# Another written order of TensorE's units in the mixer of a two-layer trunk

## The chip, the cores and the metric

The kernel runs on one core of one Trainium2 chip. The metric is the device time of one execution in microseconds (us), taken as the median of several. Engines are TensorE (PE; its weight loads are PEld), VectorE (DVE), ScalarE (ACT), GpSimd (POOL) and SyncE (SP), which issues most transfers. Each engine works through its own queue of instructions in order, and the queues wait for each other by semaphores.

## The reference

Two layers over 512 tokens of width 1024. Layer 0 has a mixer of two halves: an S5 state-space group and a stick-breaking attention with 8 heads of 64. Layer 1 is a convolution module. Both are followed by a layer norm and a feed-forward part. The change touches the mixer of layer 0 alone:

```python
h = x @ mix_w_in[i] + mix_b_in[i]
u, q, k, v = jnp.split(h, [S5_WIDTH, S5_WIDTH + SB_WIDTH, S5_WIDTH + 2 * SB_WIDTH], axis=-1)
s5_out = s5_mixer(u, ...)       # diagonal complex recurrence, gelu, gated product
sb_out = stick_breaking_attention(q.reshape(head_shape), k.reshape(head_shape), v.reshape(head_shape))
mix = jnp.concatenate([s5_out, sb_out], axis=-1) @ mix_w_out[i] + mix_b_out[i]
...
# stick-breaking attention, for each block of queries
z = jnp.einsum('bqhd,bkhd->bhqk', q_blk.astype(jnp.float32), kf) * scale
strict = key_pos[None, :] < q_pos[:, None]
log_beta = jax.nn.log_sigmoid(z)
log_keep = jnp.where(strict, jax.nn.log_sigmoid(-z), 0.0)
after = lax.cumsum(log_keep, axis=3, reverse=True) - log_keep
weights = jnp.where(strict, jnp.exp(log_beta + after), 0.0)
return jnp.einsum('bhqk,bkhd->bqhd', weights, vf)
```

## The kernel before

Activations lie transposed, features on the 128 partitions and the 512 tokens along the row. Large products are made from two-part splits: a value is kept as hi and lo, and each product of 128 x 128 by 128 x 512 is done three times (hi x hi, hi x lo, lo x hi). A projection of 128 columns therefore has 8 x 3 = 24 products (`gemm`, L219 to L227). The splitting of weights takes a cast on ACT (whi, L98 or L101) and a subtraction on DVE (wlo, L99 or L102); the raw weights come by SP (L71). Three slots hold split weights in the mixer, and a unit's weights are prepared up to two units ahead, with high priority.

The mixer is cut into units, and `ORDER` (L53) is the list of them. The loop at L798 goes through the list; it chains every TensorE instruction behind the one before it in the list (L804 to L808), so TensorE's order is written out by hand. The instructions of the other engines follow from the same tracing: a scheduler orders each of their queues by the order of tracing and by readiness, and hands out the buffers. So the list moves them too, though less strictly. The list also gives the order in which weights are fetched (L238 to L245).

The units:

- `q0` to `v3`: projection of head pair 0 to 3 (two heads each), into one of three shared PSUM banks ("mm"); ACT moves the result to SBUF (L644). There are two tiles of q, two of k and one of v.
- `aNs` with A, B or C: scores z of pair N for key blocks 0 (A), 1 and 3 (B), or 2 (C), both heads, into two of four "z" banks (L683). Behind them ACT takes the absolute value, exponential and logarithm, DVE combines (sp), POOL masks, and ACT and DVE split (sh, sl). The split tiles of A are single, those of B and C double, so one per head.
- `aNw` with A, B or C and the head: TensorE adds the running sums of the splits to z (L708), ACT takes the exponential into a w tile (three of them, tag "wt", shared with `yf`), POOL masks it (L672). A needs the splits of A, B and C, B those of B and C, and C those of B and C; the products with a block's own split come last.
- `aNt`: v transposed (vt, one tile); `aNv` with A, B or C: weighted values, L723, into the only bank "av"; `aNe`: the split of av into ch (ACT) and cl (DVE), tiles that the output projection reads.
- `G0` to `G3`: tables of a quarter of the S5 groups: DVE makes Gx and Cx, TensorE transposes (gp, L522) and multiplies (tp, L532), ACT copies to gt and tk, and SP lays tk out as Tx with sixteen copies (L539). `s`: states; TensorE makes vR and vI from gt (L547, L549), DVE runs the scan over tiles that share six places (tag "sp") and ends with the two halves of Sx. `y`: outputs yp from Tx, Cx and Sx (L577, L579), which DVE adds to U.
- `e0` to `e3`: gelu (ACT with the Tanh table, DVE), out and back through HBM by five transfers on SP (yf), and a split. A table of ACT is loaded whenever the kind of function changes in the order of tracing.
- `r`: clears a tile `rows` on POOL (it shares the six "sp" places) and loads the bias and norm vectors into it with fourteen loads on SP (L628); `R`: transposes it.
- `l0` to `l3`: gated product of S5; `o0` to `o7`: the first half of the output projection (acmo), with the result added to X by DVE.

Behind the mixer comes `tail_norm_lead` (L1019): the other half of the output projection, from the attention's splits (tiles `tla`), the sum and mean for the layer norm (`sa` on DVE, `mpa` on TensorE, L915), then the feed-forward part. Its weight buffers take memory that the mixer gives back.

## Time and profile before

| what | value |
|---|---|
| median of 3 runs | 1202.27 us (1202.24 to 1204.54) |
| the profiled execution | 1201.93 us, span 1200.2 us |
| TensorE busy | 1166.2 us of the span |
| VectorE, ScalarE, GpSimd busy | 755.8, 505.5, 61.4 us |
| mean granted TensorE clock | 0.988 |

The span is the time from the first to the last instruction of the profiled execution. The profile lists each engine's idle time by what ended it ("z1C <- ACT sh1B" is a TensorE instruction that writes z1C and started when ACT's sh1B was there), and it gives the share of full speed that TensorE's clock was granted in any stretch of time (PEclk). Names of tiles are the program's; z0A is the score tile of pair 0, blocks A.

### The profile page before, as it was taken

Reading aid. Unit: us, or ns where it says so; the run is one execution under the profiler, and the core shown is the slowest. Engines: PE = TensorE matmul, PEld = TensorE weight load, DVE = VectorE, ACT = ScalarE, POOL = GpSimd, SP = SyncE. Lnnn points to the kernel's source line nnn. Section 1 sums busy time; section 2 is a strip of 40 time slices with the busy share of each in tenths; the row PEclk is TensorE's granted clock in tenths of the full one; section 3 lists DMA queues with packets and bytes.
Section 4 is the critical chain, followed back from the end, with each engine's and each line's share of the span. In section 5 each row is a group of like instructions: output and inputs, shape, how many; then the busy total and the mean of one; then the engine's idle time right before and its main releaser. Section 6 shows DMA issues by size and latency. Waiting matters only on the chain.

```text
span 1200.2 us, 17726 instructions
## 1 busy us (share of the span) xinstructions
PE 1166.2 (97%) x7148; PEld 973.7 (81%) x7148; DVE 755.8 (63%) x1342; ACT 505.5 (42%) x798; POOL 61.4 (5%) x125
## 2 busy tenths in 40 slices
PE   9998999999999999999999999899999999999997
PEld 7776877789888888888899776599988888888885
DVE  7997885478635545545555899887843434444446
ACT  6854779334524424425323132553642331423220
POOL 1021111000000000000021110002000000000000
PEclk9998999999999999999999999999999999999999
DMA  8611321150778787887554642206142241323211
GB/s 203 177 43 31 88 67 62 53 176 17 265 249 279 260 281 265 269 288 260 183 170 158 235 140 72 73 1 211 55 146 81 93 134 57 120 74 120 70 53 70
DMA packets 132546, 169.58 MB, mean 141 GB/s; under 512 B 13874, under 2 KB 105778, under 8 KB 132464
## 3 DMA queue, kind: packets, MB, share of 16 engines
q1 hardware_dynamic: 123664, 136.96, 35.3%
q0 software_dynamic: 8640, 31.46, 7.7%
q8 instruction: 56, 0.92, 0.3%
q14 instruction: 26, 0.21, 0.1%
q10 hardware_dynamic: 160, 0.03, 0.0%
HBM read 132.12 MB, written 35.65 MB: 140 GB/s over the span
## 4 chain that ended last, share of the span: by engine, by line
PE 74%; DVE 9%; DMA 7%; issue 4%; ACT 4%; POOL 1%; SPq 0%; DVEq 0%; ACTq 0%; POOLq 0%
PE f L225 16%; PE g L1311 12%; PE acf L225 9%; PE fl L225 5%; DMA raw<-in_ffn_w_dram 5%; PE tld L225 4%; PE tlb L225 4%; PE pv L225 3%; PE h L1295 3%; DVE wlo L102 3%; PE pg L225 3%; PE cw L1126 2%; PE acmo L225 2%; PE pl L225 2%; ACT whi L101 1%
## 5 line engine op out<-in xcount | busy, mean ns | idle before, releaser
L102 DVE TENSOR_TENSOR wlo<-raw,whi 128x1024 fp32r<-128x1024 f32 x176 | 213.2, 1224 | 200.4 <-ACT whi L101 197.9
L101 ACT CAST whi<-raw 128x1024 fp32r<-128x1024 f32 x176 | 181.9, 1049 | 326.0 <-PE g L1311 106.9
L1311 PE MATMUL g<-whi,hl 128*128 128x512 f32 x208 | 81.6, 392 | 0.0
L1311 PE MATMUL g<-whi,hh 128*128 128x512 f32 x208 | 81.6, 392 | 0.0
L1311 PE MATMUL g<-wlo,hh 128*128 128x512 f32 x208 | 81.5, 392 | 0.0
L225 PE MATMUL f<-xah,whi 128*128 128x512 f32 x208 | 81.0, 390 | 0.0
L225 PE MATMUL f<-xdh,whi 128*128 128x512 f32 x208 | 81.0, 389 | 0.0
L225 PE MATMUL f<-xdh,wlo 128*128 128x512 f32 x208 | 80.9, 389 | 0.0
L225 PE MATMUL f<-xal,whi 128*128 128x512 f32 x208 | 80.9, 389 | 0.0
L225 PE MATMUL f<-xdl,whi 128*128 128x512 f32 x208 | 80.9, 389 | 0.0
L225 PE MATMUL f<-xah,wlo 128*128 128x512 f32 x208 | 80.9, 389 | 0.0
L225 PE MATMUL acf<-hl,whi 128*128 128x512 f32 x192 | 75.5, 393 | 0.2 <-DVE hl L216 0.2
L225 PE MATMUL acf<-hh,whi 128*128 128x512 f32 x192 | 75.6, 394 | 0.0
L225 PE MATMUL acf<-hh,wlo 128*128 128x512 f32 x192 | 75.4, 393 | 0.0
L215 ACT CAST hh<-fr 128x512 fp32r<-128x512 f32 x64 | 39.7, 621 | 60.6 <-DVE fr L353 60.6
L216 DVE TENSOR_TENSOR hl<-fr,hh 128x512 fp32r<-128x512 f32 x64 | 44.1, 690 | 31.8 <-ACT hh L215 31.7
L357 DVE SCALAR_TENSOR_TENSOR cy<-hp,wdw,cy 128x512 f32<-128x512 f32 (+1 forms) x81 | 52.2, 646 | 0.0
L353 DVE TENSOR_TENSOR fr<-fr 128x512 f32<-128x512 f32 x64 | 43.7, 685 | 13.4 <-ACT fr L154 13.4
L357 DVE SCALAR_TENSOR_TENSOR cz<-hp,wdw,cz 128x512 f32<-128x512 f32 (+1 forms) x74 | 47.6, 644 | 0.0
L1311 PEld LDWEIGHTS g<-whi,hl 128*128 128x128 f32 x208 | 39.0, 188 | 8.7
L1311 PEld LDWEIGHTS g<-wlo,hh 128*128 128x128 f32 x208 | 39.1, 188 | 8.7
L1311 PEld LDWEIGHTS g<-whi,hh 128*128 128x128 f32 x208 | 39.0, 188 | 8.8
(631 smaller groups left out, 2874.5 us busy)
## 6 DMA issues: line engine op xcount, KB each, us to landing
raw<-in_ffn_w_dram SPq DMA_DIRECT2D x48, 1024.0 KB, 5.5
raw<-in_ffn_w_dram SPq DMA_DIRECT2D x32, 512.0 KB, 3.6
kepth<-whi SPq DMA_DIRECT2D x30, 512.0 KB, 5.9
keptl<-wlo SPq DMA_DIRECT2D x30, 512.0 KB, 10.4
whi<-kepth POOLq DMA_DIRECT2D x30, 512.0 KB, 3.5
wlo<-keptl POOLq DMA_DIRECT2D x30, 512.0 KB, 4.6
raw<-in_conv_w_pw_dram SPq DMA_DIRECT2D x12, 1024.0 KB, 6.3
raw<-in_mix_w_in_dram SPq DMA_DIRECT2D x16, 512.0 KB, 4.8
```

Source lines behind the costliest of these rows:

```text
L101: i0 = nc.scalar.copy(hi, raw).ins
L102: i1 = nc.vector.tensor_sub(lo, raw, hi.bitcast(F32)).ins
L215: i0 = S.copy(hi, src).ins
L216: i1 = V.tensor_sub(lo, src, hi.bitcast(F32)).ins
L225: ins = PE.matmul(ps[:, c0:c1], u[:, k, ksl], v[:, c0:c1], start=start and k == 0 and i == 0, stop=stop and k == n - 1 and i == 2).ins
L353: V.tensor_tensor(o, x, y, op=op)
L357: V.scalar_tensor_tensor(o, x, s, y, op0=op0, op1=op1)
L1126: PE.matmul(cps[j, c0][g][C, :], Ds[j][t // 16][R, t % 16, :], hps[j][R, t + c0 : t + c1], start=t < 4, stop=t >= n - 4, tile_position=(R. ...
L1295: PE.matmul(ps, u, v, start=k == 0 and i == 0, stop=k == nk - 1 and i == 2)
L1311: PE.matmul(pss[b], u, v[:, kk, :], start=k + kk == 0 and i == 0, stop=k + kk == nb - 1 and i == 2)
```

## The change

The list of units gets another order. The units are the same and each is unchanged.

- Pair 0: `a0sB` and `a0sC` stand together, with `a0t`, `q1`, `k1`, `y0` behind them; then the weighings `a0wB0 a0wC0 a0wC1 a0wB1`, and `a0sA` behind these rather than between.
- `r` moves ahead of `G1`.
- `a0wA1` and `a0vB` directly follow `v1`; `a1sC`, `a1sB` and `y1` come after; `q2` and `a0vA` precede both `a1wC0` and `a1wC1`.
- `k2` goes ahead of `v2`, with `a1wB0`, `a0e` and `a1t` between; `y2`, `a1vB` and `e1` go ahead of `a1wA0`, `a2sB` ahead of `a1wA1`.
- `a2vC` goes ahead of `a2sA`.
- `a3vB`, `a3vA`, `a3e` go ahead of `o6` and `o7`.

The diff, with the lists broken into lines and the common beginning and the common stretches left out:

```diff
 q0 k0 v0 G0 s0 a0sB
-q1 a0sC k1 a0t y0 a0wC0 a0wC1 a0sA a0wB0 a0wB1 a0vC G1 s1 a0wA0 v1 a1sC a0wA1 a0vB r a1sB y1 a0vA a1wC1 q2 a0e a1wC0
+a0sC a0t q1 k1 y0 a0wB0 a0wC0 a0wC1 a0wB1 a0sA a0vC r G1 s1 a0wA0 v1 a0wA1 a0vB a1sC a1sB y1 q2 a0vA a1wC0 a1wC1
 e0 G2 a1sA s2
-a1t v2 k2 a1wB0 a1wB1 a1wA0 a1vC e1 y2 a1wA1 a2sB a1vB q3
+k2 a1wB0 a0e a1t v2 a1wB1 a1vC y2 a1vB e1 a1wA0 a2sB a1wA1 q3
 a1vA a1e e2 G3 a2sC s3 k3 a2wB1 a2t a2wC0 a2wC1
-a2sA a2wB0 a2vC
+a2vC a2sA a2wB0
 R y3 e3 v3
 ...
 o0 o1 o2 o3 o4 o5
-o6 o7 a3vB a3vA a3e
+a3vB a3vA a3e o6 o7
```

## The prediction

> **What bounds the kernel now.** I read the page's shares first, then TensorE's waits over the whole run, then busy time and granted clock in stretches laid around the longest waits, and last the order of time at each of them.

> ```profile
> span 1200.2 us, 17726 instructions
> PE 1166.2 (97%) x7148; PEld 973.7 (81%) x7148; DVE 755.8 (63%) x1342; ACT 505.5 (42%) x798; POOL 61.4 (5%) x125
> ```

> TensorE is busy for 97% of the span. So work of another engine counts only where TensorE waits for it. The waits (total, times, longest):

> ```profile
> PE z1C L708 <- ACT sh1B L215: 2.9, 1, 2.9
> PE av L723 <- POOL w2C L672: 2.5, 1, 2.5
> ...
> PE vR L547 <- ACT gt L524: 1.9, 2, 1.0
> ...
> PE z0A L683 <- ACT w0C L160: 1.4, 1, 1.4
> PE tla L225 <- DVE cl L216: 1.4, 1, 1.4
> ...
> PE mpa L915 <- DVE sa L353: 0.8, 1, 0.8
> PE v L225 <- DVE m L353: 0.6, 1, 0.6
> ```

> Five of these seven lie in the mixer; tla and mpa stand just behind it. A written order can take away such waits and nothing else, since every multiplication stays. The clock makes some of them dearer than they look:

> ```profile
> core 0: us, PE busy (x) PEld busy (x) DVE busy (x) ACT busy (x) POOL busy (x), PEclk, DMA share, GB/s
> 76.00:84.00 8.00, 7.25 (x48) 5.44 (x48) 7.31 (x16) 5.33 (x12) 1.76 (x5) 0.79 0.22 66
> 82.00:103.00 21.00, 19.73 (x132) 14.45 (x128) 19.59 (x35) 11.09 (x25) 4.44 (x10) 1.00 0.14 38
> 105.00:114.00 9.00, 7.71 (x22) 6.16 (x23) 5.97 (x13) 1.32 (x3) 0.36 (x1) 0.62 0.00 0
> 164.00:172.00 8.00, 5.46 (x39) 4.16 (x37) 6.34 (x15) 6.15 (x10) 1.24 (x4) 1.00 0.24 70
> 241.00:247.00 6.00, 4.62 (x26) 4.63 (x27) 1.18 (x2) 1.36 (x2) 0.00 (x0) 0.72 0.82 268
> 322.00:600.00 278.00, 277.69 (x1271) 229.68 (x1270) 146.93 (x165) 109.99 (x129) 0.00 (x0) 1.00 0.76 261
> ```

> The width times what is missing from the clock is what a stretch lost to it: 8 x 0.21 = 1.68 us behind the wait of z0A, 9 x 0.38 = 3.42 behind that of z1C, 6 x 0.28 = 1.68 behind that of tla. The 2.5 us of waiting in 164:172 cost no clock. The second row shows the danger: VectorE is busy for 19.59 of 21 us there, so TensorE can't run far ahead of it.

> **The change, part by part.** No instruction is added or removed. The rows of the places (start, duration, instruction, idle time before it):

> ```profile
> 76.75 1.40 PE L683 MATMUL z0A<-q,k 64*128 64x512 f32 x4 [1.45 <-ACT w0C L160]
> 98.11 1.13 PE L683 MATMUL z1B<-q,k 64*128 64x384 f32 x6 [0.31 <-ACT w0A L160]
> 99.17 0.49 PE L577 MATMUL yp<-U,Tx 128*128 128x128 f32 x2
> ...
> 102.05 1.08 PE L723 MATMUL av<-w0A,vt 128*64 128x512 f32 x4
> 105.99 0.43 PE L708 MATMUL z1C<-sh1B,negs 128*128 128x128 f32 x1 [2.86 <-ACT sh1B L215]
> 106.71 0.48 PE L708 MATMUL z1C<-sl1B,negs 128*128 128x128 f32 x1 [0.30 <-DVE sl1B L216]
> ...
> 164.39 0.33 PE L708 MATMUL z2B<-sh2B,negs 128*128 128x128 f32 x1
> ...
> 165.57 0.65 PE L723 MATMUL av<-w2C,vt 128*64 128x256 f32 x2
> 168.76 0.65 PE L723 MATMUL av<-w2C,vt 128*64 128x256 f32 x2 [2.54 <-POOL w2C L672]
> ...
> 242.38 0.41 PE L225 MATMUL tla<-ch,whi 128*128 128x256 f32 x1 [1.40 <-DVE cl L216]
> ```

> *Pair 0: both early scores, then a0t, q1, k1, y0; the weighings B0 C0 C1 B1; then a0sA.* Before, a0sA asked for two score banks right behind the two C weighings and waited 1.45 for the exponential of w0C. After, the first two banks come free behind B0 and C0, and C1 and B1 stand between. One B weighing takes 1.18 (164.39 to 165.57) and with C1 covers the wait. Gone: 1.45 + 1.68 = **3.13**. Two things are late next. q1 takes the bank of vR two units earlier than k1 did, so VectorE must have read it: between 0 and one 128x512 operation of 0.69 (row of cl, below); 0.1, because the reads of vR are the first that VectorE does there. And a0wB0 wants the B and C splits of its head together: between 0 and one weight split of 1.23 (row of wlo, below) in front of them on VectorE; 0.4, since two projections and y0 lie in between, but VectorE is full.

> *a0wA1 and a0vB ahead of a1sC and a1sB; q2 and a0vA ahead of a1wC0 and a1wC1.* Before, the C weighing of pair 1 had y1 and a0vA as cover, 99.17 to 103.13; sl1B came at 106.71, 7.5 after the scores' end at 99.24. After, y1 (2.9), a whole projection and a0vA (1.1) stand there. A projection has 24 products, at the pace of the row below (21.80 for 96) 5.45:

> ```profile
> 215.99 21.80 PE acmo L225 x96
> ```

> 2.9 + 5.45 + 1.1 = 9.4 covers 7.5 with 1.9 to spare. Gone: 2.86 + 0.30 + 3.42 = **6.58**. The 0.31 of z1B goes too, as a0vB now frees the tile for w0A's exponential ahead of the scores: **0.31**. Next late is y1, which TensorE reaches some 2.5 earlier. It wants both Sx, the end of VectorE's chain of s1, and the sixteen Tx copies of SP:

> ```profile
> 97.44 0.67 DVE L353 TENSOR_TENSOR Sx<-m,n 128x508 f32<-128x508 f32 x1
> 85.67 10.78 SPq L539 DMA_DIRECT2D Tx<-tk  x16
> DMA to landing us min/median/max: 1.7/1.8/3.2
> 96.55 0.47 SPq L628 DMA_DIRECT2D rows<-in_s_b_glu_dram  x1
> 95.23 0.31 POOL L620 MEMSET rows<- 128x256 f32 x1 [5.24 <-DVE m L353]
> ```

> Sx ended at 98.11 and y1 began at 99.17, so y1 may wait between 0 and 1.5 (2.5 less that 1.06); VectorE's chain starts earlier as well, so 0.5. The small products tp of G1 and G2 need Cx from VectorE: between 0 and a split of 1.23 in front of it; 0.5 each, near the middle as VectorE's load is high in G1 and lower in G2.

> *r ahead of G1.* One clear on POOL and fourteen loads on SP (at 0.47, some 6.6 us) now stand ahead of s1's tiles and of the Tx copies, and keep one of the six shared tiles longer. I cost it at nothing: the rows tile can take a place that s0 has left, the loads fit into the time before tk exists, and s1's chain reuses its own tiles in order. If that cover is gone, it is the worst rival below.

> *k2 ahead of v2, with a1wB0, a0e and a1t between; y2, a1vB, e1 ahead of a1wA0; a2sB ahead of a1wA1.* The loads and splits of k2 and v2 swap with their units, each prepared units ahead: 0. The projection behind s2 no longer takes vR's bank, since k2 comes first and takes that of tp: the wait of v on m, **0.56** by the order of time (0.6 above), goes. The Tanh of e1 moves ahead of w1A's exponentials; the table loads stay as many, its five transfers on SP follow it as before, and w1A is first needed behind q3: 0. a1wA1 has only a2sB (1.1, as z1B's row) between itself and a1wA0, whose end frees the single tile of sh1A: a cast and a subtraction, about twice 0.69, lie on that path, so between 0 and 1.4; its A part is the last of its products, so 0.3. The two waits of vR for gt (1.0 each) stay, as nothing was put between tp and vR.

> *a2vC ahead of a2sA.*

> ```profile
> 162.88 0.41 ACT L160 ACTIVATE w2C<-z2C 128x256 f32<-128x256 f32 x1
> ...
> 167.39 0.36 ACT L160 ACTIVATE w2C<-z2C 128x256 f32<-128x256 f32 x1
> ```

> The second exponential came only behind the first value product (165.57) and all of sp2A. There are three w tiles, and by the code yf2 and a w2B can hold two of them, so it needed the place that this product frees. Now sp2A isn't in front, but no scores cover anything either: an estimated 0.5 for the first mask, and 1.1 for the second exponential (0.36), mask and handing over. 1.6 in place of 2.54: **0.94**; between -0.5 (both heads pay in full) and 2.54 (a tile is free).

> *a3vB, a3vA, a3e ahead of o6, o7.*

> ```profile
> 239.90 1.07 PE L723 MATMUL av<-w3A,vt 128*64 128x512 f32 x2 [0.25 <-POOL w3A L672]
> 241.63 0.69 DVE L216 TENSOR_TENSOR cl<-av,ch 128x512 fp32r<-128x512 f32 x1 [3.12 <-ACT ch L215]
> ...
> 241.42 8.95 DMA raw<-in_ffn_w_dram
> ...
> 260.45 1.23 DVE wlo L102
> 261.67 0.34 DVE sa L353
> ```

> The split of the last head pair now runs under o6 and o7, 24 products or 5.45: 1.40 + 1.68 = **3.08** goes; the 0.25 stays. By the code tla's first product reads an earlier pair's ch, and it waited for cl all the same: for the bank of av, then, which o6 and o7 don't use. The FFN's first load was issued as a3vA ended (240.97), and the chain leads from it through a split at 260.45 to sa and mpa's wait. It starts 5.45 earlier against tla now, so mpa's **0.79** (0.8 above) goes.

> Sum: 3.13 + 6.58 + 0.31 + 0.56 + 0.94 + 3.08 + 0.79 = 15.4 gone; new waits 0.1 + 0.4 + 0.5 + 0.5 + 0.5 + 0.3 = 2.3, with bounds of 0 and 7.4 (0.69 + 1.23 + 1.5 + 1.23 + 1.23 + 1.4). In G1 or G2 a wait for Cx and one for gt can now fall together, 0.5 + 1.0, as long as the 1.45 that cost a clock: half of 1.68, 0.9. Net 12.2. The profiled execution took 1201.93 (span 1200.2), 0.34 below the median of 1202.27: 1189.7 against it, and 1202.27 - 12.2 = **1190** for the median.

> **Rivals.**

> 1. *A good part is given back.* VectorE sets the pace up to y1: the new waits come near their upper ends (+5.1) and trip the clock once or twice more (to 3.4): 1194 to 1199. For it: 19.59 of 21. Against: the 1.4 that VectorE idles there is partly a wait for scores that come earlier now.

> 2. *The low clock isn't the waits' doing and stays.* Then 1.68 + 3.42 + 1.68 = 6.8 stays: 1197. For it: the 2.54 before av cost no clock. Against: each of the three low stretches holds a wait of 1.40 or more, and 82:103, whose waits are 1.0 and less, kept a full clock. [...]

> 3. *Slower: the row loads block SP.* If the rows tile gets its place only from s1's chain, as before (cleared behind DVE m at 95.2, so about 93 now), and its loads stand ahead of the Tx copies in SP's order, then 93 + 6.6 + 10.8 + 1.8 lands Tx at 112.2; y1, reached at 96.7, waits 15.5, and a clock loss like that behind z1C, 3.4, follows: 1190 + 19 = 1209. It ends slower than before from a wait of 9 on. Against: r is written ahead of s1 now, so it asks for its place first.

> 4. *No change: the weight stream behind the mixer sets the end*, and TensorE waits there for what it has gained: 1201 to 1203. For it: 261 GB/s and 0.76 of the queues in 322:600. Against: TensorE lacks 0.31 in 278 there, and the first loads start earlier too.

> **Chances.** Forecast (1187 to 1194) 0.54; rival 1 0.17; rival 2 0.05; below 1187 0.05; rival 4 0.08; rival 3 0.07; another in-order mishap that ends slower 0.04. Faster by over 0.2% (2.4 us, about what a measurement here can tell from no change) 0.81, within 0.08, slower 0.11. The range goes down by the new waits (2.3), the clock (0.9) and the rest of a2vC (1.6) to 1185.2, and up through rivals 1 and 2 to 1200.

> **What would show it.** Right: TensorE's waits of z1C, z0A, tla, v on m and mpa are missing, av on w2C is near 1.6, the clock is full in the mixer, and tla starts about 10 earlier (the terms up to a2vC and the 1.40, less the new waits and 0.9). Wrong: a wait of yp on Tx or Sx, of tp on Cx, a low clock at new places, row loads ahead of Tx in SP's order with a long wait before them, or waits in 322:600 that have grown from 0.3.

## The result and the profile after

The changed kernel takes 1191.39 us (median of 4 runs, 1188.93 to 1193.48) against 1202.70 for the kernel before beside it (4 runs, 1202.24 to 1204.54): ratio 0.9902, 95% interval 0.9879 to 0.9925, so 11.8 us less, between 9.0 and 14.5. The profiled execution took 1188.93, the lowest of the four; its span is 13.0 below the span of before.

The page after, first lines:

```profile
span 1187.2 us, 17722 instructions
PE 1158.6 (98%) x7148; PEld 969.0 (82%) x7148; DVE 754.7 (64%) x1342; ACT 506.7 (43%) x798; POOL 67.0 (6%) x125
```

TensorE, VectorE and ScalarE have as many instructions as before. TensorE's busy time fell by 7.6 all the same: a product lasts longer at a low clock (one form of fl takes 0.28 at 273.12 and 0.41 at 273.57 before, where the clock falls in between), and there is less low clock, 13.65 us outside the program's end where there were 23.89 (the sums stand under e3). TensorE's waits after (in total, times, longest), those that bear on the argument:

```profile
PE av L723 <- POOL w2C L672: 2.1, 2, 1.2
PE vI L549 <- ACT gt L524: 2.0, 1, 2.0
...
PE av L723 <- DVE cl L216: 1.5, 1, 1.5
...
PE tla L225 <- DVE X L357: 0.9, 1, 0.9
...
PE vR L547 <- ACT gt L524: 0.4, 1, 0.4
```

Waits for z1C, z0A, v on m and mpa no longer stand in the list. New are vI on gt, av on cl, and tp on Cx; tla waits for something else than before. Busy time and granted clock (PEclk) in the same stretches as before, with two others (83 to 91, 760 to 776):

```profile
83.00:91.00 8.00, 7.06 (x31) 6.41 (x31) 6.27 (x11) 2.17 (x5) 1.58 (x3) 0.79 0.07 16
82.00:103.00 21.00, 19.06 (x105) 16.16 (x106) 19.14 (x35) 10.73 (x22) 6.21 (x8) 0.92 0.12 34
105.00:114.00 9.00, 8.62 (x66) 5.97 (x65) 8.67 (x19) 8.27 (x14) 1.39 (x3) 1.00 0.23 69
241.00:247.00 6.00, 6.00 (x52) 6.00 (x51) 5.78 (x12) 2.00 (x2) 0.00 (x0) 1.00 0.67 200
322.00:600.00 278.00, 278.00 (x1331) 232.91 (x1330) 146.02 (x171) 106.71 (x126) 1.21 (x2) 1.00 0.74 252
760.00:776.00 16.00, 14.52 (x86) 11.86 (x72) 13.56 (x37) 8.95 (x21) 0.00 (x0) 0.68 0.00 1
```

The clock is full where z1C and tla used to wait, but a low stretch stands at 84 to 87.5, behind the new wait of vI, and 760 to 776 lost 16 x 0.32 = 5.1 us. The places in order of time (start, duration, instruction, idle time before it), first TensorE's, then the rows of ACT, VectorE and SP that explain them:

```profile
80.28 0.43 PE L532 MATMUL tp<-Cx,Gx 128*32 128x128 f32 x8 [1.17 <-DVE Cx L357]
83.94 1.33 PE L549 MATMUL vI<-U,gt 128*128 128x128 f32 x5 [2.04 <-ACT gt L524]
127.78 0.65 PE L723 MATMUL av<-w1C,vt 128*64 128x256 f32 x4 [1.47 <-DVE cl L216]
156.09 0.65 PE L723 MATMUL av<-w2C,vt 128*64 128x256 f32 x2 [0.90 <-POOL w2C L672]
157.92 0.65 PE L723 MATMUL av<-w2C,vt 128*64 128x256 f32 x2 [1.19 <-POOL w2C L672]
234.35 0.35 PE L225 MATMUL tla<-ch,whi 128*128 128x256 f32 x1 [0.87 <-DVE X L357]
```

```profile
82.78 0.62 ACT L215 CAST sh0A<-sp0A 128x512 fp32r<-128x512 f32 x1 [1.57 <-POOL sp0A L672]
83.31 0.58 ACT L524 COPY gt<-gp 128x512 f32<-128x512 f32 x1
126.95 0.68 DVE L216 TENSOR_TENSOR cl<-av,ch 128x512 fp32r<-128x512 f32 x1
74.31 0.27 SPq L628 DMA_DIRECT2D rows<-in_conv_b_pw_dram  x1
84.08 10.98 SPq L539 DMA_DIRECT2D Tx<-tk  x16
```

ACT idled 1.57 for the mask of sp0A with the second copy of gt queued behind that cast, so vI waited 2.04. The subtraction of a0e (cl) now stands deep in VectorE's chain of s2, and the value products of a1vC need the one bank of av that it reads. The fourteen row loads (the last one shown) were issued by 74.6, long before the Tx copies, which follow at 84.08.

### The profile page after: what moved, and what is told of

The parts are those of the page before. It is cut to its first block, busy times and chain, and to the rows that moved or that the text cites. A ratio compares the mean times of both kernels' runs of the same rounds, so it can differ in the third digit from the quotient of the medians.

```text
span 1187.2 us, 17722 instructions
## 1 busy us (share of the span) xinstructions
PE 1158.6 (98%) x7148; PEld 969.0 (82%) x7148; DVE 754.7 (64%) x1342; ACT 506.7 (43%) x798; POOL 67.0 (6%) x125
## 4 chain that ended last, share of the span: by engine, by line
PE 82%; DVE 8%; ACT 4%; DMA 3%; issue 1%; SPq 1%; POOL 0%; DVEq 0%; ACTq 0%; POOLq 0%
PE f L225 23%; PE g L1311 12%; PE acf L225 11%; PE tld L225 4%; PE tlb L225 4%; PE fl L225 3%; PE pv L225 3%; PE h L1295 3%; PE pg L225 3%; PE cw L1126 2%; PE tla L225 2%; PE acmo L225 2%; PE pl L225 2%; DVE wlo L102 1%; DMA raw<-in_ffn_w_dram 1%
## 5 line engine op out<-in xcount | busy, mean ns | idle before, releaser
L102 DVE TENSOR_TENSOR wlo<-raw,whi 128x1024 fp32r<-128x1024 f32 x176 | 213.3, 1223 | 199.7 <-ACT whi L101 197.5
L225 PE MATMUL f<-xah,whi 128*128 128x512 f32 x208 | 81.0, 390 | 0.0
L225 PE MATMUL f<-xdh,whi 128*128 128x512 f32 x208 | 81.0, 389 | 0.0
L225 PE MATMUL f<-xdh,wlo 128*128 128x512 f32 x208 | 80.9, 389 | 0.0
L225 PE MATMUL f<-xal,whi 128*128 128x512 f32 x208 | 80.9, 389 | 0.0
L225 PE MATMUL f<-xdl,whi 128*128 128x512 f32 x208 | 80.9, 389 | 0.0
L225 PE MATMUL f<-xah,wlo 128*128 128x512 f32 x208 | 80.9, 389 | 0.0
L225 PE MATMUL acf<-hl,whi 128*128 128x512 f32 x192 | 75.6, 394 | 0.0
L225 PE MATMUL acf<-hh,whi 128*128 128x512 f32 x192 | 75.6, 394 | 0.0
L225 PE MATMUL acf<-hh,wlo 128*128 128x512 f32 x192 | 75.4, 393 | 0.0
L215 ACT CAST hh<-fr 128x512 fp32r<-128x512 f32 x64 | 39.7, 620 | 59.0 <-DVE fr L353 59.0
L216 DVE TENSOR_TENSOR hl<-fr,hh 128x512 fp32r<-128x512 f32 x64 | 44.1, 690 | 31.1 <-ACT hh L215 31.1
L353 DVE TENSOR_TENSOR fr<-fr 128x512 f32<-128x512 f32 x64 | 43.7, 685 | 14.4 <-ACT fr L154 14.4
L88 POOL DMA_DIRECT2D whi<-kepth x30 | 16.1, 536 | 556.8 <-PE tlb L225 386.3
```

The source lines that it names most:

```text
L88: nc.gpsimd.dma_start(x, d)
L102: i1 = nc.vector.tensor_sub(lo, raw, hi.bitcast(F32)).ins
L215: i0 = S.copy(hi, src).ins
L216: i1 = V.tensor_sub(lo, src, hi.bitcast(F32)).ins
L225: ins = PE.matmul(ps[:, c0:c1], u[:, k, ksl], v[:, c0:c1], start=start and k == 0 and i == 0, stop=stop and k == n - 1 and i == 2).ins
L353: V.tensor_tensor(o, x, y, op=op)
```

## The experiments

Each ratio is to the kernel before, run beside it; the interval is 95%.

**e1_tail_only: the tail's move alone, on the kernel before.**

```diff
-o5 o6 o7 a3vB a3vA a3e
+o5 a3vB a3vA a3e o6 o7
```

> Before, with a3vB a3vA a3e ahead of o6 and o7 and nothing else. What the changed kernel showed at this place: tla waits 0.87 for VectorE's X in place of 1.40 for cl, no low clock behind it (1.68), no wait of mpa (0.79), and also no wait of fl for xah (1.78 before) and no low clock behind that (another 1.7). Theory A, all of these belong to this move: 0.53 + 1.68 + 0.79 + 1.78 + 1.7 = 6.5 faster, 1196. Theory B, the wait for xah went for another reason (the earlier start against the clock's own windows, or the front's shift): 0.53 + 1.68 + 0.79 = 3.0, 1199.7, with fl still waiting near 272. Rival, the low clock is not the waits' doing: 1.3 or less, 1201.4.

Measured: 1197.24 (5 runs), ratio 0.9958 (0.9946 to 0.9970), or 5.0 us, between 3.6 and 6.5. The time lies between theory A (1196) and theory B (1199.7). The profile shows A: fl waits no longer.

**e2_no_tail: the changed kernel with the tail as before.** (The diff is that of e1, reversed.)

> The changed kernel with o6 and o7 put back ahead of a3vB a3vA a3e. TensorE reached tla 8.03 earlier in the changed kernel, 0.53 of it by the tail's own wait, so the rest of the change is worth 7.5: 1195 against before, if nothing is given back behind the mixer. Theory A (the tail move also took the wait for xah): 1191.4 + 6.5 = 1198, that is only 4.8 better than before, which would need something given back. Theory B (xah's wait went with the earlier arrival): 1191.4 + 3.0 = 1194.4 and no wait for xah here.

Measured: 1197.80 (6 runs), ratio 0.9966 (0.9953 to 0.9979), 4.1 us, between 2.5 and 5.7. That is theory A again, and fl waits 1.78 here as before.

So the tail is worth about half. By its time alone it can't be told from the prediction's 3.87, but the traces show another way to it. Count of tla's products on TensorE ahead of mpa and behind it (two stretches each, cut at mpa's start), before and then in e1:

```profile
242.30:262.00 19.70, 18.90 (x143) 18.70 (x143) 4.30 (x10) 0.91 0.73 233
262.00:272.00 10.00, 6.56 (x49) 6.15 (x49) 2.22 (x5) 1.00 0.19 65
```

```profile
242.80:256.70 13.90, 13.66 (x112) 13.46 (x112) 3.73 (x9) 1.00 0.64 191
256.70:268.60 11.90, 10.11 (x80) 9.87 (x80) 2.22 (x5) 1.00 0.21 71
```

Behind the mixer the order isn't written out, and the scheduler put mpa behind 143 of tla's products before (in e2 too), behind 112 in e1 (in the changed kernel too). With 80 rather than 49 left behind mpa, they cover the norm's way to xah: fl starts 10.1 behind mpa before and in e2, each time after that wait, and 11.8 behind it in e1 and in the changed kernel, with none. The first product of the feed-forward part, before and in e1:

```profile
272.13 0.74 PE L225 MATMUL fl<-xah,whi 128*128 128x256 f32 x4 [1.78 <-ACT xah L154]
```

```profile
268.60 0.40 PE L225 MATMUL fl<-xah,whi 128*128 128x256 f32 x2
```

The 1.78 is gone. The low clock at 273 is gone too, but it can't be put down to that wait: e2, and e4 and e9 below, have the same 1.78 and no low clock behind it. They have tla's 1.40 as well, and none behind that either.

**e3_filler: the waits of z1C and tla filled with idle work.** The kernel before, with 24 transposes of the identity ahead of a1wC1 and 12 behind a3e, each time into one of the three shared "mm" banks, where nobody reads them.

```diff
-y1 a0vA a1wC1 ... a3vA a3e
+y1 a0vA f24 a1wC1 ... a3vA a3e f12
+    def filler(n):
+        ps = mm("fill")
+        for _ in range(n):
+            PE.transpose(ps[:, :P], ident, ident)
```

> Before, in its own order, with 24 transposes of a constant (128x128, some 0.11 us each, 2.7 in all) between a0vA and a1wC1, and 12 (1.3) behind a3e: they fill the waits of z1C (2.86) and tla (1.40) with work that nobody reads. The waits stay, only TensorE isn't idle in them. If idleness lowers the clock, the two low stretches go and 3.42 + 1.68 = 5.1 is won: 1197.6, with the same ends of the waits. If the low clock isn't the waits' doing, nothing is won, 1202.7, or up to 0.5 lost where the filling overruns. [...]

Measured: 1203.86 (11 runs), ratio 1.0011 (1.0000 to 1.0022): nothing gained. The two stretches are at full clock, and others aren't:

```profile
105.00:114.00 9.00, 8.53 (x52) 7.21 (x51) 7.85 (x17) 2.56 (x6) 1.11 (x3) 1.00 0.01 1
164.00:176.00 12.00, 9.42 (x44) 7.83 (x44) 6.96 (x20) 6.42 (x11) 1.24 (x4) 0.72 0.15 46
241.00:247.00 6.00, 5.69 (x37) 4.07 (x36) 1.18 (x2) 2.28 (x3) 0.29 (x1) 1.00 0.48 154
```

Cut exactly on the low stretches outside the program's end (where TensorE is idle), the view gives their number and length; the sums of five stretches before, of three in e3 and of two in the changed kernel:

```profile
sum 23.89, PE 23.59 PEld 20.73 DVE 17.72 ACT 11.21 POOL 0.36; mean PE 4.72 PEld 4.15 DVE 3.54 ACT 2.24 POOL 0.07
```

```profile
sum 23.89, PE 22.18 PEld 18.42 DVE 17.21 ACT 14.65 POOL 2.31; mean PE 7.39 PEld 6.14 DVE 5.74 ACT 4.88 POOL 0.77
```

```profile
sum 13.65, PE 13.65 PEld 12.60 DVE 11.47 ACT 6.01 POOL 0.91; mean PE 6.83 PEld 6.30 DVE 5.74 ACT 3.00 POOL 0.46
```

In e3 it is the same 23.89 us at 0.50: a low stretch of 6.83 in place of 3.41 behind z0A, one behind w2C's wait of 2.55, which had cost no clock before, and a longer one behind tld's waits (777.95 to 788.19). The single runs agree: their mean granted clock is 0.9885 over e3's eleven and 0.9893 over the 23 of the kernel before. Nor is the place of a low stretch fixed by the order. e1 and e9 leave the front as it was, and in both profiles the low clock behind z0A lasts 6.8 us (before: 3.4) and the one behind z1C 3.4 (before: 6.8), at waits of nearly the same length (1.45; 2.74 and 2.98 for 2.86). And at the tail there was nothing to win by the clock, as mpa shows in the kernel before, e3, e4 (below) and e1, each with SP's issue of the last projection load (it goes out as a3vA ends), before and in e1:

```profile
241.00 0.37 SPq L71 DMA_DIRECT2D raw<-in_mix_w_out_dram  x1
262.06 0.70 PE L915 MATMUL mpa<-sa,ones 128*128 128x256 f32 x2 [0.79 <-DVE sa L353]
```

```profile
264.13 0.70 PE L923 MATMUL mpa<-sa,ones 128*128 128x256 f32 x2 [2.28 <-DVE sa L353]
```

```profile
259.00 0.70 PE L915 MATMUL mpa<-sa,ones 128*128 128x256 f32 x2 [1.76 <-DVE sa L353]
```

```profile
236.27 0.37 SPq L71 DMA_DIRECT2D raw<-in_mix_w_out_dram  x1
256.76 0.70 PE L915 MATMUL mpa<-sa,ones 128*128 128x256 f32 x2 [0.30 <-DVE sa L353]
```

With the old tail mpa begins 21.1 us behind that issue (262.06 - 241.00; in e2, e4, e9 21.0 to 21.1, in e3 21.2), whatever TensorE gained in between: its wait for sa grows instead. In these profiles only an earlier issue moves it.

**e4_front_only: the order up to a1wC1 alone** (a0e stays behind a0vA), on the kernel before.

```diff
-q0 k0 v0 G0 s0 a0sB q1 a0sC k1 a0t y0 ... y1 a0vA a1wC1 q2 a0e a1wC0
+q0 k0 v0 G0 s0 a0sB a0sC a0t q1 k1 y0 ... y1 q2 a0vA a0e a1wC0 a1wC1
```

> Before, with the changed order up to a1wC1 only (r ahead of G1 included; a0e directly behind a0vA, as before); from e0 on the old order. In the changed kernel a1wC ended at 108.0 in place of 116.1, 8.1 earlier, its new waits (tp 1.17, vI 2.04 with a low clock) included. Theory, a TensorE-bound kernel keeps what it gains: 8.1 faster, 1194.6. Rival, VectorE or the weight stream takes a part back later: less than 5, 1197.7 or more, with new or longer waits behind e0. The prediction's own sum for these parts was 10.0 less 2.0 of new waits and 0.9 of clock, 7.1.

Measured: 1200.30 (12 runs), ratio 0.9974 (0.9962 to 0.9986), 3.1 us, between 1.7 and 4.6: the rival. vR of G2 starts 7.1 earlier (112.74 against 119.88), but SP's issue at a3vA's end only 3.0 (237.97 against 241.00). Between them:

```profile
117.00 0.47 PE L225 MATMUL v<-x0h,whi 128*128 128x512 f32 x1 [1.77 <-DVE m L353]
162.83 0.69 PE L723 MATMUL av<-w2C,vt 128*64 128x256 f32 x1 [2.55 <-POOL w2C L672]
```

v's wait grew from 0.56 to 1.77, as VectorE's reads of vR came only 5.9 earlier (115.57 against 121.49), and this time a low stretch followed w2C's wait, 10 x 0.34 = 3.4 lost:

```profile
160.00:170.00 10.00, 7.45 (x34) 6.28 (x33) 4.80 (x15) 4.34 (x8) 1.24 (x4) 0.66 0.18 55
```

**e9_mid_only: the middle alone**, on the kernel before (a0e stays where it was).

```diff
-a1t v2 k2 a1wB0 a1wB1 a1wA0 a1vC e1 y2 a1wA1 a2sB a1vB q3
+k2 a1wB0 a1t v2 a1wB1 a1vC y2 a1vB e1 a1wA0 a2sB a1wA1 q3
-a2sA a2wB0 a2vC
+a2vC a2sA a2wB0
```

> The kernel before with only the middle of the new order: k2 ahead of v2, y2, a1vB and e1 ahead of a1wA0, a2sB ahead of a1wA1, a2vC ahead of a2sA. Theory: the middle by itself is worth its two waits, 0.56 (v on m) and 0.5 to 0.9 (w2C): 1202.9 - 1.3 = 1201.6. The rest of the whole change's gain, 11.3 less 5.5 (tail alone) and 2.7 (front alone), is then what the middle brings only once the front runs earlier: the front alone was stopped by the very waits (v on m 1.77, w2C 2.55 with 3.4 of low clock) that the middle removes. Rival: the parts add up, and the middle alone brings the missing 3 us: 1199.8.

Measured: 1201.89 (11 runs), ratio 0.9993 (0.9983 to 1.0003): 0.8 us, as expected for the middle by itself; the rival's 3 us fall. The theory's second half isn't borne out either: front and middle together (e2, which moves a0e too) brought 4.1, the two alone 3.1 + 0.8 = 3.9. Nothing extra shows between them, though the intervals leave room for some 2.5 either way. All three parts sum to 8.9, the whole to 11.8 (9.0 to 14.5). The granted clock of the single runs tells where the other 2.9 lie: its mean is 0.9893 before, 0.9904 in e1, 0.9895 in e2 and 0.9928 in the four runs of the changed kernel. What is missing from 1, times the span, is about 4 us less for the whole and about 1.7 less for e1 and e2 together. Whether that belongs to the whole order or to these four runs stays open.

**e5_a0e_early, e6_a2wC_first, e7_v1_first: on the changed kernel, one step upon the other.**

```diff
e5: -y1 q2 a0vA a1wC0 a1wC1 e0 G2 a1sA s2 k2 a1wB0 a0e a1t
    +y1 q2 a0vA a0e a1wC0 a1wC1 e0 G2 a1sA s2 k2 a1wB0 a1t
e6: -a2wB1 a2t a2wC0 a2wC1 a2vC
    +a2wC0 a2wC1 a2t a2wB1 a2vC
e7: -r G1 s1 a0wA0 v1 a0wA1 a0vB a1sC a1sB y1 q2
    +r v1 G1 s1 a0wA0 a1sC a0wA1 a0vB a1sB q2 y1
```

> The changed kernel with a0e back directly behind a0vA, the rest of the new order kept. Theory: the new wait of 1.47 us before the first products of a1vC (on DVE's cl, in the single av bank) exists because a0e was written behind s2 and so its subtraction queued behind s2's chain. With a0e early the wait is gone from the trace and vR of G2 and the projections behind it stand about 1.5 us earlier against the start. Time: 1191.4 - 1.5 = 1189.9. Rival: as in the run with the front alone, what is gained before pair 2 is lost again at later waits (v on m, the second w2C mask with its clock, mpa on sa), so the wait is gone and the time stays at 1191.4 within 0.7 us.

> The kernel e5 with the order a2wC0 a2wC1 a2t a2wB1 a2vC a2sA a2wB0 in pair 2, so that both C weighings come before the B weighing of the other head. Theory: the second exponential of w2C waited for a free tile (the value product of the first head); with a2wB1 behind both C weighings a tile is free, both masks are under way while TensorE does a2t and a2wB1, and the wait of 2.09 us before the value products of C falls below 0.5. Time 1.6 us below e5: 1188.3. Rival: not the tile but the chain of scores, exponential and mask itself is late; then the wait moves to the splits in front of a2wC and the total of waits in pair 2 stays at 2 us, with the time of e5.

> The kernel e6 with v1 ahead of G1, a1sC ahead of a0wA1, and q2 ahead of y1, so that a whole projection covers Cx's preparation, and A weighings cover the second copy of gt. Theory: TensorE's waits for Cx (1.17 us) and for the second gt (2.04 us) with the low clock behind them (half of 3.41, 1.7 us) are the front's remaining price, and fall below 1.0 in sum. Time 3 us below e6: 1185.3. Rival: VectorE sets the pace from s0 to y1, so that the same 3 us turn up as waits elsewhere before pair 2 (y1 on Sx, a1wC on the splits), and the time is that of e6 within 0.7 us or above it.

Measured: e5 1194.18 (6 runs), ratio 0.9924 (0.9902 to 0.9945); e6 1189.73 (5), 0.9895 (0.9882 to 0.9908); e7 1193.76 (6), 0.9918 (0.9900 to 0.9936). In e5 the wait for cl is gone, but y2's first product waits 0.60 for Tx a little later and the time is no better: the rival. In e7, no faster than e6, the two waits in G1 fell from 3.2 to 0.62, but G2 got 1.34, 1.29 and 1.89 for VectorE's Gx and Cx, which waited nowhere before: its rival, VectorE sets the pace up to y1 and beyond. e6 came out 4.5 below e5 where 1.6 was expected (their intervals overlap), but its profile looked like a miss:

```profile
155.63 4.86 POOL L672 TENSOR_SCALAR_AFFINE_SELECT w2C<-w2C 128x128 f32<-128x128 f32 x2 [4.20 <-ACT w2C L160]
159.83 1.41 PE L723 MATMUL av<-w2C,vt 128*64 128x256 f32 x3 [3.64 <-POOL w2C L672]
```

Both exponentials were early, but POOL's first mask took 4.14 of those 4.86 (0.44 in the changed kernel), beside VectorE operations back to back.

**e8_mask_on_pe and e10_after_mask_on_pe: w2C's mask made by TensorE**, in e6's order and in that of the changed kernel.

```diff
+    V.tensor_scalar(cf, cf, 30000.0, None, ALU.mult)
...
+            onpe = p == 2 and g[0] == "C"
+                if onpe:
+                    PE.matmul(zs[g][:, o : o + P], ident, cf, start=False, stop=False, skip_group_check=True)
-            ws_[g] = w_, mask(w_, g)
+            ws_[g] = w_, None if onpe else mask(w_, g)
```

> The kernel e6 with the mask of w2C made by TensorE: a product of the identity with a triangle of -30000 is added to z2C before the exponential, and POOL's two masks on w2C are left out. In e6 the first of these masks took 4.14 us while VectorE ran operation after operation with two inputs in SBUF; in the changed kernel the same mask took 0.44. Theory: POOL's mask was held up by VectorE, and so TensorE's 3.64 us in front of the value products and the low clock of 158.6 to 165.5 are this mask's price. Without it the wait is below 0.4 and vR of G3's successors and tla stand 3.5 us or more earlier against the start than in e6; time 1189.7 - 3.5 = 1186.2, less up to 1.7 of clock. Rival: the gain is used up by later waits, as in the run with the front alone and in e5 (the projection behind s3, w3A, mpa on sa): the time stays at 1189.7 within 0.7 us.

> The changed kernel, its order untouched, with w2C's mask made by TensorE as in e8 (a product of 128x128 added to z2C; POOL's two masks on w2C left out). It tells the price of the mask alone from that of the tile: in the changed kernel TensorE waits 0.90 for the first mask and 1.19 for the second head, whose exponential starts only behind the first value product. Theory: the first wait falls to about 0.4 and the second by the mask's 0.64 to about 0.6, 1.0 together; time 1191.4 - 1.1 = 1190.3, so that e8's 1186.4 needs both the order of e6 and the mask on TensorE. Rival: the mask is the whole price and the order of e6 adds nothing: 1186.4 here too.

Measured: e8 1186.41 (4 runs), ratio 0.9864 (0.9849 to 0.9879); e10 1188.24 (4), 0.9873 (0.9857 to 0.9890). In e8 the value products follow without a wait; in e10 the two waits of 2.09 fell to 0.47, more than the theory's 1.0. They are the two fastest versions run with an interval. That of e8 lies below that of e6 and, at its end, touches that of the changed kernel (0.9879). e8 and e10 overlap and e10 lies between its two expectations, so what e6's order adds isn't settled.

**e11_one_input and e12_e6_again: what holds the mask up.** e11 is e6 with two one-input operations in s3; e12 is e6 once more.

```diff
         tt(n1, m4, si, ALU.mult)
+        if q == 3:
+            for _ in range(2):
+                ts(n1, n1, 1.0, 0.0, ALU.mult, ALU.add)
```

> The kernel e6 with two operations added on VectorE behind the first n of s3: n times 1 in place, 128x512, one input each, 0.41 us each by the row of g<-g. Everything else is as in e6, POOL's masks included. Theory: the mask of 4.14 us was held up because each VectorE operation from 155.4 to 159.7 read two tiles of SBUF; beside an operation that reads one the mask runs. It then ends within the added pair, about 1.3 us after its start in place of 4.14, and TensorE's wait of 3.64 falls to 1.5 or less, though VectorE has 0.7 us more to do; time 1189.7 - 2 = 1187.7. Rival 1: the mask is held up by any VectorE work; then it lasts 4.8 (0.7 more) and the wait is 4.3: 1190.4. Rival 2: the second mask is held up in the first one's place by what follows (1.2 of wlo at least) and TensorE waits for it: about 2.5 us of wait stays, 1188.7.

> The kernel e6 once more, for its profile. In e11 the mask of w2C wasn't held up (0.62 us) although no operation with one input ran beside it, which speaks against the theory there. This tells whether the 4.14 us of the mask and the 3.64 of TensorE's wait belong to the program or to one execution. If to the program (for it: e7 showed 4.15 in the same place), both are there again within 0.1 us, and what e11 changed in VectorE's stream let the mask in. If to the execution, the mask takes 0.4 to 0.8, the wait in front of the value products is below 0.5, and the time is nearer to the 1189.2 to 1190.3 of e6's other runs than to the 1192.0 of its profiled one.

Measured: e11 1190.28 (6 runs, 1186.78 to 1193.81), ratio 0.9894 (0.9876 to 0.9913): not told from e6. Its mask took 0.62, but it was over before the first added operation began (156.37). So e11 tells nothing of the theory it was made for. e12, one run, 1186.95: the same program as e6, and the mask wasn't held. VectorE's operations beside the mask in e6 (three and the last of seven shown), and then POOL's masks, TensorE's products and VectorE's operations in e12:

```profile
155.43 0.66 DVE L353 TENSOR_TENSOR m<-m,tc 128x512 f32<-128x512 f32 x1
156.01 0.68 DVE L353 TENSOR_TENSOR n<-m,ts 128x512 f32<-128x512 f32 x1
156.61 1.21 DVE L102 TENSOR_TENSOR wlo<-raw,whi 128x1024 fp32r<-128x1024 f32 x1
...
159.66 0.69 DVE L353 TENSOR_TENSOR Sx<-m,n 128x508 f32<-128x508 f32 x1
```

```profile
154.27 1.30 POOL L672 TENSOR_SCALAR_AFFINE_SELECT w2C<-w2C 128x128 f32<-128x128 f32 x2 [4.20 <-ACT w2C L160]
155.09 1.18 PE L723 MATMUL av<-w2C,vt 128*64 128x256 f32 x4 [0.27 <-ACT vt L658]
154.06 0.66 DVE L353 TENSOR_TENSOR m<-m,tc 128x512 f32<-128x512 f32 x1
154.65 0.77 DVE L353 TENSOR_TENSOR n<-m,ts 128x512 f32<-128x512 f32 x1
155.34 1.30 DVE L102 TENSOR_TENSOR wlo<-raw,whi 128x1024 fp32r<-128x1024 f32 x1
```

In both the first mask starts 0.2 behind the start of the same m (155.63 against 155.43, 154.27 against 154.06). In e12 both masks are over 1.30 later, and n and wlo last 0.09 longer each than in e6; in e6 VectorE went on at its usual durations and the mask ended 4.14 later. So the hold belongs to the execution, not to the order, and e6's theory of the w tile was right where the mask got through: TensorE's wait there is 0.27, for vt.

## Why the prediction was right in sum and where it was wrong

The time forecast, 1190, is 1.4 below the measured median and within its runs. Term by term the sum is less good: errors of both signs met, and that they nearly cancelled was luck. The front was forecast at 7.1 and brought 3.1 by itself; the tail brought as much as forecast or more, in part by a step that wasn't forecast; and 2.9 arose in no part by itself. (In the prediction the upper bounds of the new waits add up to 7.3, not 7.4; nothing hangs on it.)

- **z0A, 3.13.** The 1.45 is gone. Its 1.68 of clock is not: a low stretch stands 6 us later, behind vI (8 x 0.21 = 1.7), where the sum had set aside 0.9.
- **z1C, 6.58.** Wait and low clock are gone in the profile, and vR of G2 starts 9.0 earlier (its wait of 0.98 is 0.38). But e3 filled that wait and won nothing, and the whole front won 3.1 alone. Pricing a low stretch where one profile shows it was the faulty step: with the same front it lasted 3.4 in e1 and e9, and in e3, without the wait, others had grown. The rest of the front's gain went to the waits of v and w2C (e4).
- **z1B 0.31 and v on m 0.56** went as forecast.
- **a2vC, 0.94.** 2.54 became 2.09, not 1.6: 0.45. The mask was handed over later (0.90 for 0.5), and the second head paid 1.19 for 1.1.
- **New waits in G1.** tp on Cx 1.17 for 0.5, inside its bounds. The copy of gt was the miss: "the two waits of vR for gt (1.0 each) stay" overlooked ACT's queue, where a0sA's cast, now later, stands ahead of the second copy. 2.04 in place of 0.96.
- **a0e behind s2, costed at 0.** The single av bank was named for the tail and forgotten here: 1.47. e5 shows that removing it gains nothing measurable: 0.60 comes back at once as a wait for Tx.
- **y1, q1, a0wB0, a1wA1, tp of G2**: 1.8 in the sum, none above 0.1 in the trace.
- **tla, 3.08, and mpa, 0.79.** The tail's 3.87 was forecast; e1 measured 5.0 (3.6 to 6.5). tla still waits 0.87, for o7's addition into X, so av's bank was not all that it needed. By mpa's 21.1 us behind the load's issue the 1.68 of clock was worth nothing by itself, and e2, e4 and e9 don't show it. What the traces of e1 show in its place is the load's issue, 4.7 earlier (236.27 against 241.00), and the missed step: the scheduler's new place for mpa, behind which the 1.78 before fl is gone.
- **tla's start** came 8.0 earlier (242.38 to 234.35), forecast about 10; 5.0 more came behind it, where 2.5 was forecast (1.68 of clock and the 0.79). Between the two profiles come 1.78 of xah and 1.7 of the clock at 273 to these, and 1.7 goes off, since 760 to 776 lost 5.1 where the like stretch before lost 3.4 (by the same view); some 0.7 behind isn't traced.

Of the rivals, the first (a good part given back) describes what happened up to a3vA: e2's 1197.80 less the tail's forecast 3.87 is 1193.9, at the edge of its 1194 to 1199. Of its reasons only tp's wait (1.17 of 1.23) came near an upper end. The second said that low clocks aren't the waits' doing. e3 gives it half: every low stretch in the mixer sits at a wait (before 1.45 and 2.86, after 2.04), but filling two waits moved low stretches and kept their sum of 23.89. Yet in the changed kernel the sum fell to 13.65, and its runs have the higher clock, so this rival's 1197 was wrong. The third fell plainly: the row loads were issued by 74.6. The fourth fell for its stretch, as 322 to 600 shows TensorE busy for all 278.00; but at mpa, with the old tail, a load did take back what TensorE had gained.

## What to carry to other kernels

When a written order is changed, follow not only the unit moved but the queues of the other engines: what is now traced ahead of whom on ACT and VectorE (here a cast ahead of gt's second copy: vI waited 2.04), and which single bank or tile its end frees (here av's: 1.47). Before crediting a wait, look for the next point that is tied to something else (here mpa, with the old tail 21.1 us behind a load's issue): what is won ahead of it is lost at it, unless the issue moves too. Low clocks are better priced by their sum over a run, and over several runs, than where one profile shows them (here 23.89 us before and in e3, at other places).

## What was unexpected of the hardware

*POOL's mask beside VectorE.* The same two 128x128 masks took 1.30 in e12 and 4.86 in e6 (4.14 of it the first), one program, with VectorE two-input operations back to back in both. In e12 two of these operations, n and wlo, lasted 0.09 longer each than in e6 (0.77 for 0.68, 1.30 for 1.21); in e6 the first mask lasted beside five of them in a row (n to the second n, 156.01 to 159.63) at 0.67 to 0.68, and 1.21 for wlo. That VectorE held the mask is read from this coincidence; no experiment shows it, nor by what means. That the mask's delay was TensorE's 3.64 is shown by e8, where the mask is left out, and by e12, where it wasn't held: the wait is gone in both.

```profile
164.11:167.52 3.41, 2.11 (x11) 1.30 (x10) 3.38 (x6) 3.35 (x7) 0.00 (x0) 1.00 0.40 116
167.52:170.93 3.41, 2.17 (x16) 1.79 (x17) 2.85 (x10) 2.32 (x4) 1.24 (x4) 1.00 0.16 47
```

```profile
158.81:162.22 3.41, 1.47 (x9) 0.94 (x8) 3.38 (x7) 2.98 (x6) 0.00 (x0) 1.00 0.51 158
```

Before, TensorE was busy for 0.55 to 2.02 us of the piece ahead of each of the five low stretches. From these numbers I estimate that the idle time within one piece counts, and with it where a wait falls on the grid. This is read from the profiles afterwards and wasn't tested, and the bound isn't sharp (the changed kernel has pieces with 1.95 and 1.92 busy, 125.05 to 128.47 and 155.77 to 159.19, e4 one with 1.64, 114.44 to 117.85, and a full clock behind each; e7 one with 3.11, 768.30 to 771.71, and a low clock). This widens what a single profile can mislead by: a profile with two such pieces fewer looks 3.4 us better (2 x 3.41 x 0.50).
